# A bias carried in the idle rows of another matmul: forget-gate rows moved into the second score pass of a two-layer attention trunk

## The chip, the cores and the metric

The kernel runs on one core of one Trainium2 chip. The metric is device time in microseconds for one execution of the whole program. Where a difference is told in per cent, it is a difference of medians of such times.

## The reference, cut to what matters

Two layers run over 512 tokens of width 1024. Each layer projects the residual stream into four groups of heads (4 heads of width 64 each), mixes tokens in each group, normalises and projects the result back, and then applies a gated feed-forward block. The group that matters here is A, forgetting attention: a causal softmax whose score for query t and key s has the sum of the log forget gates between s and t added to it.

```python
log_f = jax.nn.log_sigmoid(fgate + fox_b_f[l])
cum = jnp.cumsum(log_f, axis=1).transpose(0, 2, 1)
...
s = jnp.einsum('bqhd,bkhd->bhqk', qi, k) * scale
s = s + cq[..., :, None] - cum_log_f[..., None, :]
s = jnp.where(kpos[None, :] <= qpos[:, None], s, NEG_INF)
p = jax.nn.softmax(s, axis=-1)
```

Groups B (latent attention), C (stick-breaking attention) and D (windowed attention) have no such bias.

## The kernel before, in words

**Precision by splitting.** Every matmul operand is held as a high part, rounded to the matmul's input type, and a low part, the remainder. A product of two such numbers takes three partial products: high by high, high by low, low by high.

**Scores in two passes.** A head is 64 wide and the TensorE array has 128 rows, so groups A, C and D pack two of the partial products into one pass. A q tile holds the high part of head i on rows 64i to 64i+63 and the low part on the other 64 rows. A `k` tile holds the low part of k against q's high part, and the high part of k against q's low part: the first pass gives both mixed products. A `kh` tile holds the high part of k on the head's own 64 rows and zeros on the other 64: the second pass, with the same q tile as the other operand, gives high by high. The zeros are written once, at the start of the program (L2205). There are three `kh` tiles in a ring, and five pairs of heads in a layer use them in turn (one for D, two each for C and A).

**The third pass of group A.** `gates()` computes the running sum of log gates for the four heads and splits it. It leaves two 128-row tiles, `augq` and `augk`, with 32 rows for each head, whose product over those rows is the bias cum[t] - cum[s]. Four copies of `augq`, one a head (`augh0` to `augh3`, L1100, on GpSimd), keep only the rows of their head. `group_a()` hands `causal_group` an extra operand pair, and each block of scores gets one more matmul: `augh` of the head by `augk`.

**Blocks.** A causal head is scored in four query blocks of 128 queries against 128, 256, 384 and 512 keys, in three groups (b=0 has the first two blocks, b=1 the third, b=2 the fourth). Each group's first pass is followed by a pass that adds the mask (`maskb` by `identb`). Softmax follows on VectorE (row maximum, L1433), ScalarE (exponential, L1443) and GpSimd or ScalarE (scaling, L1418 or L1416), then a transpose on TensorE (L1555) and its evacuation (L1361, L442), and the product with v.

**The order of the work.** The program plans itself: a list scheduler with estimated costs picks, engine by engine, what is issued next, and every engine then runs its instructions in that order. Attention tasks come before dense work (projections) in priority, so dense matmuls fill TensorE where attention is not ready. `copy()` (L717) picks ScalarE or GpSimd, whichever the planner believes will end first. Score groups are started in the order D, C, A, B, and only the first of the list is looked at, so B's scores are not started before A's last.

**Pairs.** Heads 0 and 1 of A are pair 0 (`fq0`, `fk0`), heads 2 and 3 are pair 1 (`fq1`, `fk1`). In layer 0 the dense order has `fk0`, ..., `fq0`, ..., `fq1`, `fk1`, then the latent queries (`q`) and the output projections; in layer 1 `fq0` and `fk0` come earlier. `q_evac` (L911, L444) and `k_evac` (L924, L442, and `copy`) move a pair out of PSUM.

Of the kernel before, what the change touches and what calls it, by code (L numbers as in the profile page):

```python
# [25 lines left out]
ALU = mybir.AluOpType  # L26
# [3 lines left out]
P = 128  # L30
S = 512
# [15 lines left out]
GA, GB, GC, GD = range(4)  # L47
# [18 lines left out]
E_PE, E_ACT, E_DVE, E_POOL, E_SP = range(5)  # L66
# [8 lines left out]
NOW = (0.0,) * 5  # L75


def join(*deps):

    if any(x is None for x in deps):  # L80
        return None
    return tuple(map(max, zip(*deps))) if len(deps) > 1 else deps[0]
# [18 lines left out]
def c_pool(n):  # L101
    return 245.0 + 0.832 * n
# [17 lines left out]
class Sched:  # L120
# [9 lines left out]
    def spawn(self, gen, prio=0, order=None):  # L130
        self.n += 1
        self.step((gen, prio, self.n if order is None else order), None)
# [220 lines left out]
def trunk(ctx: ExitStack, tc: tile.TileContext, d):  # L353
    nc = tc.nc
    ACT, DVE, POOL, PE = nc.scalar, nc.vector, nc.gpsimd, nc.tensor
    engines = {E_ACT: ACT, E_DVE: DVE, E_POOL: POOL}
    sched = Sched()
    spawn = sched.spawn
# [47 lines left out]
    amask = const.tile([P, 10], F32, name="amask")  # L406
# [30 lines left out]
    f = f32  # L437
# [279 lines left out]
    def copy(out, in_, n, dep, prio=None, psum=None):  # L717

        e_ = sched.best(dep, (E_ACT, c_act(n, psum is not None)), (E_POOL, c_pool(n)))[0]
        e = yield Op(e_, c_act(n, psum is not None) if e_ == E_ACT else c_pool(n), dep, prio)  # L720
        if e_ == E_ACT:
            ACT.copy(out=out, in_=in_ if psum is None else psum)  # L722
        else:
            POOL.tensor_scalar(out=out, in0=f(in_), scalar1=1.0, scalar2=0.0, op0=ALU.mult, op1=ALU.add)
        return e
# [138 lines left out]
    def layer(l):  # L864
        w_in = d["w_in"][l]
        qk = {}
# [3 lines left out]
        at = {}  # L870
# [185 lines left out]
        def gates():  # L1056
            e = yield lambda: join(at["gate"].dep, at["vec"], r_u.ready(), r_temp.ready(2)) if "gate" in at and "vec" in at else None
            gate, bf = small["gate"], vec["bf"]
            u = r_u.take()
            t0, t1 = r_temp.take(), r_temp.take()  # L1060
            gp = u.tile
            e = yield Op(E_PE, 4 * 107.0, join(e, u.dep))
            for t in range(NT):
                PE.transpose(out=gp[:, t * P:(t + 1) * P], in_=gate[:, t].rearrange("p h c -> p (h c)"), identity=ident)
            small["gate_h"].give(e)
            lg = [t0.tile, t1.tile]
            a = yield Op(E_ACT, c_act(S, True, 1), join(e, t0.dep))
            ACT.activation(out=lg[0], in_=gp, func=AF.Abs, bias=bf)
            b = yield Op(E_DVE, c_dve(S) + 61.0, join(e, t1.dep))
            DVE.tensor_scalar(out=lg[1], in0=gp, scalar1=bf, scalar2=0.0, op0=ALU.add, op1=ALU.min)  # L1070
            u.give(join(a, b))
            a = yield Op(E_ACT, c_act(S, False), a)
            ACT.activation(out=lg[0], in_=lg[0], func=AF.Exp, scale=-1.0)
            a = yield Op(E_ACT, c_act(S, False, 1), a)
            ACT.activation(out=lg[0], in_=lg[0], func=AF.Ln, bias=ones[:, 0:1])
            e = yield Op(E_DVE, c_dve(S), join(a, b))
            DVE.tensor_tensor(out=lg[1], in0=lg[1], in1=lg[0], op=ALU.subtract)
            e = yield Op(E_DVE, c_dve(S, 2.083), e)
            DVE.tensor_tensor_scan(out=lg[0], data0=lg[1], data1=lg[1], initial=0.0, op0=ALU.add, op1=ALU.bypass)
            augq, augk = (sb.tile([P, S], F32R, name=n, tag=n, bufs=1) for n in ("augq", "augk"))  # L1080
            heads = [sb.tile([P, S], F32R, name=f"augh{h}", tag=f"augh{h}", bufs=1) for h in range(4)]
            a = yield Op(E_ACT, c_act(S, False), e)
            ACT.copy(out=augq, in_=lg[0])
            e = yield Op(E_DVE, c_dve(S), a)
            DVE.tensor_tensor(out=lg[1], in0=lg[0], in1=f(augq), op=ALU.subtract)
            e = yield Op(E_DVE, c_dve(S, 0.52), e)
            DVE.tensor_copy(lg[0], f(augq))
            for aug, k in ((augq, 0), (augk, 3)):
                e = yield Op(E_DVE, c_half(S), e)
                DVE.tensor_scalar(out=aug, in0=lg[0], scalar1=amask[:, k:k + 1], scalar2=amask[:, k + 2:k + 3], op0=ALU.mult, op1=ALU.add)  # L1090
                e = yield Op(E_DVE, c_dve(S) + 61.0, e)
                DVE.scalar_tensor_tensor(out=aug, in0=lg[1], scalar=amask[:, k + 1:k + 2], in1=f(aug), op0=ALU.mult, op1=ALU.add)
                if aug is augq:
                    q_done = e
            t0.give(e)
            t1.give(e)
            hs = []
            for h in range(4):
                g = yield Op(E_POOL, c_pool(S), q_done)
                POOL.tensor_scalar(out=heads[h], in0=f(augq), scalar1=amask[:, 6 + h:7 + h], scalar2=0.0, op0=ALU.mult, op1=ALU.add)  # L1100
                hs.append(g)
            small["aug"] = heads, augk
            at["aug"] = join(e, *hs)


        def kv_norm(dep):
# [272 lines left out]
        def qk_pairs(q, i, k, kh, half):  # L1379

            return ((q[:, i], k[:, half]), (q[:, i], kh[:, half]))
# [39 lines left out]
        def softmaxes(scale=None):  # L1421
            def normed(ps, blocks, w, dep):

                p, nb = w[0].tile, len(blocks)
                r = sm.tile([P, 8], F32, name="smx", bufs=8)
                sl, c = [], 0
                for _, n in blocks:
                    sl.append(slice(c, c + n * P))
                    c += n * P
                dep = join(dep, w[0].dep)  # L1430
                for j, s_ in enumerate(sl):
                    e = yield Op(E_DVE, c_dve(s_.stop - s_.start), dep)
                    DVE.tensor_reduce(out=r[:, j:j + 1], in_=ps.tile[:, s_], op=ALU.max, axis=AX, negate=True)  # L1433
                nm = 0
                if scale is not None:
                    i0 = blocks[0][0]
                    e = yield Op(E_DVE, 72.0, join(e, at["rsq"]))
                    DVE.tensor_tensor(out=r[:, 2:2 + nb], in0=r[:, 0:nb], in1=scale[:, i0:i0 + nb], op=ALU.mult)
                    nm = 2
                for j, s_ in enumerate(sl):  # L1440
                    i = blocks[j][0]
                    a = yield Op(E_ACT, c_act(s_.stop - s_.start, True, 2 if scale is None else 3), e)
                    ACT.activation(out=p[:, s_], in_=ps.tile[:, s_], func=AF.Exp, bias=r[:, nm + j:nm + j + 1],  # L1443
                                   scale=1.0 if scale is None else scale[:, i:i + 1], accum_out=r[:, 4 + j:5 + j])
                ps.give(a)
                e = yield Op(E_DVE, 75.0, a)
                DVE.reciprocal(out=r[:, 6:6 + nb], in_=r[:, 4:4 + nb])
                out = []
                for j, s_ in enumerate(sl):
                    out.append((yield from normalize(p[:, s_], r[:, 6 + j:7 + j], s_.stop - s_.start, e)))  # L1450
                return w[0], join(*out)
            return normed
# [132 lines left out]
        def use_qk(key, held, n, dep):  # L1585
            held = held if isinstance(held, tuple) else (held,)
            qk_uses.setdefault(key, Joint(n, lambda dep: [h.give(dep) for h in held])).add(dep)

        def operands_2(qn, kn, more=None):

            def operands(h):
                pair, i = divmod(h, 2)
                if ((qn, pair), i) not in qk or ((kn, pair), i) not in qk or (more and more not in at):
                    return None
                (q, a, half), ((k, kh), b, _) = qk[(qn, pair), i], qk[(kn, pair), i]
                return qk_pairs(q.tile, i, k.tile, kh.tile, half), join(a, b, at[more] if more else NOW)

            def free(h, dep):
                pair, i = divmod(h, 2)
                for n in (qn, kn):  # L1600
                    use_qk((n, pair), qk[(n, pair), i][0], 6, dep)

            return operands, free
# [3 lines left out]
            return causal_group(GC, operands, None, 1, stick, "c", "vc", 2, free)  # L1607

        def group_a():
            operands, free = operands_2("fq", "fk", "aug")  # L1610

            def extras(h, i, o):
                heads, augk = small["aug"]
                n = (i + 1) * P
                return [(o, heads[h][:, i * P:n], augk[:, :n])]

            return causal_group(GA, operands, extras, 0, softmaxes(), "a", "va", 1, free)

        def group_b():
            def operands(h):  # L1620
# [649 lines left out]
```

## Time and profile before

| | us |
|---|---|
| median of 3 runs | 1229.88 (1228.12 to 1230.49) |
| the profiled execution, whole | 1222.83 |
| its span, first to last instruction | 1221.0 |
| TensorE busy | 1186.2 (97%) |
| VectorE busy | 893.4 (73%) |
| ScalarE busy | 675.8 (55%) |
| GpSimd busy | 238.7 (20%) |

The profiled execution is one run; 1.83 us of it lie around the span, and it lies 7.05 us under the median of the three runs. Attention takes about 0 to 240 us and 610 to 845 us of the span, the two feed-forward blocks the rest. In the rows, PE is TensorE, DVE VectorE, ACT ScalarE and POOL GpSimd; all matmuls have line 464, so they are told apart by their operands.

### The profile page before, as it was taken

To read this page: it belongs to the slowest core of one execution; us is meant where nothing else is said; L and a number is where in the kernel's file an instruction comes from. 1 tells how busy PE (TensorE), PEld (TensorE's weight loads), DVE (VectorE), ACT (ScalarE), POOL (GpSimd) and SP (SyncE) were. 2 spreads that over 40 slices of the span, in tenths; PEclk is the share of its full clock that TensorE was granted. 3 is DMA by queue.
4 is the path that set the end of the run, shared out by engine and by line. 5 is a ranking of instruction groups with operands and counts; after the bars stand their busy time and mean duration, and the time that the engine had idled before them with its cause. 6 is when DMAs were issued, how large, how long until landed. Compare 5 with 4: busy or idle time off the path is not lost.

```text
span 1221.0 us, 20328 instructions
## 1 busy us (share of the span) xinstructions
PE 1186.2 (97%) x7669; PEld 1077.5 (88%) x7669; DVE 893.4 (73%) x1699; ACT 675.8 (55%) x1429; POOL 238.7 (20%) x245
## 2 busy tenths in 40 slices
PE   9999999989999999999999999999899999999996
PEld 7989878779999889998889888788799989899985
DVE  5669668799986548873665886788999956599626
ACT  4759759456654335552347687584655633256421
POOL 3552653400000000000035536643000000000001
PEclk9999999999999999999999999999999999999999
DMA  6312220413333243423233221303234341343341
GB/s 201 88 43 66 59 95 9 139 57 101 103 105 103 71 138 89 118 87 123 86 71 86 56 62 31 104 21 118 87 88 119 93 135 49 109 120 87 104 138 69
DMA packets 112162, 110.75 MB, mean 91 GB/s; under 512 B 9792, under 2 KB 94656, under 8 KB 112064
## 3 DMA queue, kind: packets, MB, share of 16 engines
q1 hardware_dynamic: 112064, 109.45, 30.0%
q8 instruction: 60, 0.98, 0.3%
q14 instruction: 38, 0.31, 0.1%
HBM read 107.34 MB, written 2.10 MB: 90 GB/s over the span
## 4 chain that ended last, share of the span: by engine, by line
PE 84%; DVE 9%; issue 3%; ACT 3%; DMA 1%; POOL 0%; SPq 0%; POOLq 0%; DVEq 0%; ACTq 0%
PE ps L464 81%; PE ps L1555 2%; DVE x_res L1741 1%; DVE qk L442 1%; DVE xT L442 1%; DVE pt L442 1%; DVE x_res L856 1%; PE ps L749 1%; DMA x_res<-in_x 1%; ACT xT L722 0%; DVE qk L444 0%; DVE temp L1304 0%; DVE augk L1090 0%; ACT kh L924 0%; PE ps L1695 0%
## 5 line engine op out<-in xcount | busy, mean ns | idle before, releaser
L464 PE MATMUL ps<-xT,w_hi 128*128 128x256 f32 (+1 forms) x1128 | 216.7, 320 | 0.0
L464 PEld LDWEIGHTS ps<-xT,w_hi 128*128 128x128 f32 x1128 | 163.2, 191 | 11.8
L464 PE MATMUL ps<-w_hi,qk 128*128 128x512 f32 (+1 forms) x560 | 171.1, 387 | 0.0
L464 PE MATMUL ps<-xT,w_lo 128*128 128x256 f32 (+1 forms) x888 | 166.5, 305 | 0.0
L722 ACT CAST w_hi<-w_raw 128x1024 fp32r<-128x1024 f32 (+2 forms) x86 | 88.0, 1023 | 109.4 <-PE ps L464 87.0
L442 POOL TENSOR_TENSOR w_lo<-w_raw,w_hi 128x1024 fp32r<-128x1024 f32 (+4 forms) x66 | 120.9, 1838 | 107.3 <-ACT w_hi L722 88.9
L442 DVE TENSOR_TENSOR w_lo<-w_raw,w_hi 128x1024 fp32r<-128x1024 f32 x47 | 57.6, 1225 | 111.5 <-ACT w_hi L722 111.4
L464 PEld LDWEIGHTS ps<-xT,w_lo 128*128 128x128 f32 x888 | 124.1, 192 | 7.5
L464 PEld LDWEIGHTS ps<-w_hi,qk 128*128 128x128 f32 x560 | 104.2, 188 | 20.8
L464 PE MATMUL ps<-w_hi,mix 128*128 128x512 f32 x352 | 110.0, 393 | 4.8 <-DVE xT L442 3.5
L464 PE MATMUL ps<-w_lo,qk 128*128 128x512 f32 (+1 forms) x280 | 108.1, 386 | 0.0
L1909 ACT COPY temp<-ps 128x256 f32<-128x256 f32 x120 | 44.8, 373 | 84.4 <-PE ps L464 83.9
L659 ACT CAST w_hi<-temp 128x512 fp32r<-128x512 f32 x78 | 48.3, 620 | 64.4 <-DVE temp L602 35.7
L770 POOL TENSOR_SCALAR x_res<-x_res 128x1024 f32<-128x1024 f32 x8 | 9.4, 1179 | 374.3 <-DVE lnst L838 357.2
L464 PEld LDWEIGHTS ps<-w_hi,mix 128*128 128x128 f32 x352 | 64.6, 188 | 18.5 <-issue 4.3
L442 DVE TENSOR_TENSOR w_hi<-temp,w_hi 128x512 fp32r<-128x512 f32 x78 | 53.4, 688 | 30.7 <-ACT w_hi L659 30.5
L659 ACT CAST w_lo<-temp 128x512 fp32r<-128x512 f32 x82 | 50.7, 621 | 43.4 <-DVE temp L602 26.0
L467 POOL TENSOR_TENSOR lnst<-lnst,mhalf 128x1 f32<-128x1 f32 x4 | 3.9, 984 | 362.0 <-DVE lnst L838 362.0
L464 PE MATMUL ps<-xT,qk 128*128 128x256 f32 x528 | 67.8, 287 | 3.2 <-DVE qk L442 3.2
L464 PE MATMUL ps<-w_lo,mix 128*128 128x512 f32 x176 | 69.0, 392 | 0.9 <-DVE pt L442 0.9
L464 PE MATMUL ps<-w_hi,xT 128*128 128x388 f32 (+1 forms) x256 | 68.9, 350 | 0.4 <-DVE qk L444 0.4
L464 PEld LDWEIGHTS ps<-xT,qk 128*128 128x128 f32 x528 | 65.3, 194 | 4.2 <-DVE qk L442 4.0
(233 smaller groups left out, 2701.6 us busy)
## 6 DMA issues: line engine op xcount, KB each, us to landing
w_raw<-in_w_down SPq DMA_DIRECT2D x44, 512.0 KB, 3.8
w_raw<-in_w_in SPq DMA_DIRECT2D x26, 512.0 KB, 3.7
w_raw<-in_w_gate SPq DMA_DIRECT2D x24, 512.0 KB, 3.7
w_raw<-in_w_up SPq DMA_DIRECT2D x24, 512.0 KB, 3.7
w_raw<-in_w_o SPq DMA_DIRECT2D x16, 512.0 KB, 3.7
vd<-in_w_up SPq DMA_DIRECT2D x10, 512.0 KB, 3.7
mixf<-in_w_up SPq DMA_DIRECT2D x10, 512.0 KB, 3.6
vd<-in_w_gate SPq DMA_DIRECT2D x10, 512.0 KB, 3.8
```

Source lines behind the costliest of these rows:

```text
L442: eng.tensor_tensor(out=lo, in0=src, in1=f(hi), op=ALU.subtract)
L464: PE.matmul(out, lhsT=lhsT, rhs=rhs, start=start, stop=stop, skip_group_check=True)
L467: POOL.tensor_tensor(out=out, in0=ve, in1=mhalf[:ve.shape[0], :ve.shape[1]], op=ALU.pow)
L659: ACT.copy(out=self.part[0], in_=src)
L722: ACT.copy(out=out, in_=in_ if psum is None else psum)
L749: PE.transpose(out=u.tile[:, k * P:(k + 1) * P], in_=x[:, t, kk * P:(kk + 1) * P], identity=ident)
L770: POOL.tensor_scalar(out=x[:, t], in0=x[:, t], scalar1=ALPHA, scalar2=0.0, op0=ALU.mult, op1=ALU.add)
L856: DVE.scalar_tensor_tensor(out=x[:, t, csl], in0=centred[c], scalar=st[:, 9:10], in1=bb[c], op0=ALU.mult, op1=ALU.add)
L1555: PE.transpose(out=u.tile[:, k * P:(k + 1) * P], in_=p.tile[:, k * P:(k + 1) * P], identity=ident)
L1741: DVE.scalar_tensor_tensor(out=x[:, t, csl], in0=ps.tile, scalar=rs[:, t:t + 1], in1=x[:, t, csl], op0=ALU.mult, op1=ALU.add, accum_out=st ...
L1909: ACT.copy(out=dst, in_=src)
```

## The change

The third pass of group A is taken out. Its rows go where the second pass had zeros: each head gets its own query tile for the second pass (`augh` of the head) with the high part of q on the head's 64 rows and the masked gate rows of its pair on the other 64, and the zero rows of the pair's `kh` tile are overwritten with the pair's 64 rows of `augk`. That takes, a head, one masked copy on GpSimd over 64 rows instead of 128, and two plain copies of 64 rows by 512 (`copy`, on ScalarE or GpSimd). The copies wait for the pair's q and k. The heads are prepared in order, inside `gates()`. When all six score groups of a pair are issued, a new task writes the zeros back with two memsets on GpSimd, and only then is `kh` given back to its ring.

```diff
             t0.give(e)
             t1.give(e)
-            hs = []
+            small["aug"] = heads
             for h in range(4):
-                g = yield Op(E_POOL, c_pool(S), q_done)
-                POOL.tensor_scalar(out=heads[h], in0=f(augq), scalar1=amask[:, 6 + h:7 + h], scalar2=0.0, op0=ALU.mult, op1=ALU.add)
-                hs.append(g)
-            small["aug"] = heads, augk
-            at["aug"] = join(e, *hs)
+                pair, i = divmod(h, 2)
+                mine, other = slice(i * 64, i * 64 + 64), slice(64 - i * 64, 128 - i * 64)
+                from_ = slice(pair * 64, pair * 64 + 64)
+                q = yield Op(E_POOL, c_pool(S), q_done)
+                POOL.tensor_scalar(out=heads[h][other], in0=f(augq[from_]), scalar1=amask[from_, 6 + h:7 + h], scalar2=0.0,
+                                   op0=ALU.mult, op1=ALU.add)
+                yield lambda: NOW if (("fq", pair), i) in qk and (("fk", pair), i) in qk else None
+                (qt, dq, _), ((_, kh), dk, _) = qk[("fq", pair), i], qk[("fk", pair), i]
+                a = yield from copy(heads[h][mine], qt.tile[mine, i], S, dq)
+                b = yield from copy(kh.tile[other, i], augk[from_], S, join(dk, e))
+                at["aug", h] = join(q, a, b)
...
         def group_a():
-            operands, free = operands_2("fq", "fk", "aug")
-
-            def extras(h, i, o):
-                heads, augk = small["aug"]
-                n = (i + 1) * P
-                return [(o, heads[h][:, i * P:n], augk[:, :n])]
-
-            return causal_group(GA, operands, extras, 0, softmaxes(), "a", "va", 1, free)
+            plain, _ = operands_2("fq", "fk")
+
+            def operands(h):
+                if ("aug", h) not in at or plain(h) is None:
+                    return None
+                pairs, dep = plain(h)
+                return (pairs[0], (small["aug"][h], pairs[1][1])), join(dep, at["aug", h])
+
+            def zeros(pair, held, dep):
+                k, kh = held
+                for i in range(2):
+                    e = yield Op(E_POOL, 470.0, dep)
+                    POOL.memset(f(kh.tile[64 - i * 64:128 - i * 64, i]), 0.0)
+                k.give(dep)
+                kh.give(e)
+
+            uses = {}
+
+            def free(h, dep):
+                pair, i = divmod(h, 2)
+                use_qk(("fq", pair), qk[("fq", pair), i][0], 6, dep)
+                held = qk[("fk", pair), i][0]
+                uses.setdefault(pair, Joint(6, lambda dep: spawn(zeros(pair, held, dep)))).add(dep)
+
+            return causal_group(GA, operands, None, 0, softmaxes(), "a", "va", 1, free)
```

`operands_2` loses its third argument, which only group A used.

## Rows read from the trace of the kernel before

**Rows 1.** The page's chain that ended last, shares of the span by engine.

```profile
PE 84%; DVE 9%; issue 3%; ACT 3%; DMA 1%; POOL 0%; SPq 0%; POOLq 0%; DVEq 0%; ACTq 0%
```

**Rows 2.** Tile `augh`, its matmuls: count, ns min/median/max, starts, forms.

```profile
L464 PE MATMUL ps<-augk,augh x32: 279/362/478, 136.6 to 792.1; 128*128 128x128 f32 x8, 128*128 128x256 f32 x8, 128*128 128x384 f32 x8, 128*128 128x512 f32 x8
```

**Rows 3.** Timeline of PE, group C scoring: start, duration, line, operands, shape, count.

```profile
91.32 0.30 PE L464 MATMUL ps<-qk,qk 128*128 128x128 f32 x1
...
91.94 0.62 PE L464 MATMUL ps<-xT,w_hi 128*128 128x512 f32 x2
...
99.27 0.40 PE L464 MATMUL ps<-qk,qk 128*128 128x512 f32 x1
...
99.86 0.54 PE L464 MATMUL ps<-w_hi,xT 128*128 128x416 f32 x2
```

**Rows 4.** Timeline of PE, group A scoring heads 0 and 1 in layer 0.

```profile
137.89 0.39 PE L464 MATMUL ps<-qk,qk 128*128 128x512 f32 x1
...
138.70 0.60 PE L1151 MATMUL ps<-ident,temp 128*128 128x128 f32 x4
139.06 0.31 PE L464 MATMUL ps<-qk,qk 128*128 128x128 f32 x1
...
139.91 0.63 PE L464 MATMUL ps<-xT,w_hi 128*128 128x512 f32 x2
```

**Rows 5.** Windows, layer 0: length; busy PE, PEld, DVE, ACT, POOL; clock; DMA; GB/s.

```profile
136.00:172.00 36.00, 36.00 (x204) 30.91 (x203) 20.64 (x49) 24.69 (x60) 20.45 (x24) 0.95 0.26 83
172.00:185.40 13.40, 11.08 (x57) 8.61 (x56) 13.16 (x20) 7.38 (x14) 7.27 (x5) 1.00 0.25 82
185.40:222.00 36.60, 35.34 (x227) 30.27 (x228) 31.10 (x94) 31.13 (x87) 16.64 (x24) 1.00 0.09 28
```

**Rows 6.** Timeline of PE where A's pairs begin, in brackets idle before and releaser.

```profile
136.37 0.31 PE L464 MATMUL ps<-qk,qk 128*128 128x128 f32 x1
...
172.07 0.30 PE L464 MATMUL ps<-qk,qk 128*128 128x128 f32 x1
...
175.15 0.63 PE L464 MATMUL ps<-qk,w_hi 128*128 128x512 f32 x2
...
183.22 0.70 PE L464 MATMUL ps<-w_hi,mix 128*128 128x512 f32 x2 [1.75 <-DVE xT L442]
```

**Rows 7.** Timeline of DVE at the ends of `fq0` and `fk1`, layer 0.

```profile
135.51 1.41 DVE L444 SCALAR_TENSOR_TENSOR qk<-ps,qk 64x512 fp32r<-64x512 f32 x2 [1.19 <-ACT qk L911]
...
171.24 1.41 DVE L442 TENSOR_TENSOR qk<-ps,kh 64x512 fp32r<-64x512 f32 x2 [4.04 <-ACT kh L924]
...
176.21 0.29 DVE L1433 TENSOR_REDUCE smx<-ps 128x1 f32<-128x128 f32 x1
```

**Rows 8.** Timeline of ACT in layer 1, evacuation of `fk0`.

```profile
704.18 1.17 ACT L924 CAST kh<-ps 64x512 fp32r<-64x512 f32 x2
```

**Rows 9.** Timeline of PE in layer 1, head 0 of group A.

```profile
730.10 0.31 PE L464 MATMUL ps<-augk,augh 128*128 128x128 f32 x1
```

**Rows 10.** Tile `kh`: the copies on POOL.

```profile
L724 POOL TENSOR_SCALAR qk<-kh x17: 612/617/671, 18.0 to 775.0; 64x512 fp32r<-64x512 f32 x17
```

**Rows 11.** Timeline of POOL, a memset.

```profile
125.97 0.53 POOL L1120 MEMSET temp<- 128x512 f32 x1
```

**Rows 12.** Timeline of DVE, one operation twice in `gates()`.

```profile
63.11 0.54 DVE L1090 TENSOR_SCALAR augq<-temp,amask 128x512 fp32r<-128x512 f32 x1
...
65.64 2.75 DVE L1090 TENSOR_SCALAR augk<-temp,amask 128x512 fp32r<-128x512 f32 x1
```

**Rows 13.** Timeline of POOL beside it.

```profile
65.69 2.41 POOL L442 TENSOR_TENSOR w_lo<-w_raw,w_hi 128x1024 fp32r<-128x1024 f32 x1 [9.02 <-ACT w_hi L722]
68.07 3.31 POOL L1100 TENSOR_SCALAR augh<-augq,amask 128x512 fp32r<-128x512 f32 x4
```

**Rows 14.** Windows of 2 us, the granted clock after POOL.

```profile
152.00:154.00 2.00, 2.00 (x10) 1.90 (x9) 0.17 (x1) 0.00 (x0) 1.91 (x3) 0.50 0.72 219
154.00:156.00 2.00, 2.00 (x10) 1.73 (x9) 1.17 (x2) 1.53 (x4) 1.94 (x2) 0.74 0.11 43
```

More of the change, by code (lines that the diff above doesn't have):

```diff
@@ L1587, in use_qk, with operands_2 @@
             qk_uses.setdefault(key, Joint(n, lambda dep: [h.give(dep) for h in held])).add(dep)
-        def operands_2(qn, kn, more=None):
+        def operands_2(qn, kn):
             def operands(h):
                 pair, i = divmod(h, 2)
-                if ((qn, pair), i) not in qk or ((kn, pair), i) not in qk or (more and more not in at):
+                if ((qn, pair), i) not in qk or ((kn, pair), i) not in qk:
                     return None
                 (q, a, half), ((k, kh), b, _) = qk[(qn, pair), i], qk[(kn, pair), i]
-                return qk_pairs(q.tile, i, k.tile, kh.tile, half), join(a, b, at[more] if more else NOW)
+                return qk_pairs(q.tile, i, k.tile, kh.tile, half), join(a, b)
             def free(h, dep):
```

## The prediction, made before the changed kernel ran

> **What bounds the kernel now.** I read the chain that ended last first: 84% of it is TensorE, 9% VectorE, 3% ScalarE [rows 1]. A change that only takes matmuls away therefore starts with a good claim to its time, if the matmuls stand where TensorE is the one that sets the pace. So the second view is the windows of the stretch in which group A is scored [rows 5]. There are three kinds of stretch. From 136 to 172 us TensorE is busy in all of 36.00 us, while VectorE has 20.64 and ScalarE 24.69: pair 0 is scored here, and TensorE is the bound. From 172 to 185.4 us TensorE has 11.08 of 13.40 and VectorE 13.16: pair 1 becomes ready here, and VectorE is the bound (it still has the rotary products of group B to do). From 185.4 to 222 us TensorE has 35.34 of 36.60, with VectorE and ScalarE at 31 each: TensorE again, but closely followed. Layer 1 repeats this at the end of its attention. The third view is the timeline of TensorE and VectorE where the two pairs begin [rows 6, 7], because the new copies stand exactly there.
>
> **What is removed.** The third pass is 32 matmuls in the whole program, 8 of each width [rows 2]. Their listed durations overlap with their neighbours, so I don't add those up. I compare start to start, the same score group with and without the pass. Group C has none: its b=0 group runs from 91.32 to the next matmul at 91.94, 0.62 us, and its b=2 group from 99.27 to 99.86, 0.59 us [rows 3]. Group A's b=0 group runs from 139.06 to 139.91, 0.85 us, and b=2 from 137.89 to 138.70, 0.81 us [rows 4]. So the pass costs 0.23 us in b=0 (widths 128 and 256 together) and 0.22 us in b=2 (width 512). For b=1 (width 384) I take 0.17 us, an estimate three quarters of the way to the 512 figure. That is 0.62 us a head, and 8 heads give 5.0 us of TensorE time.
>
> **Which part of it counts.** Pair 0 in each layer lies where TensorE is saturated: 2 heads x 0.62 x 2 layers = 2.5 us, counted in full. Pair 1 is split. The whole of head 2 and the b=0 group of head 3 (0.62 + 0.23 = 0.85 us a layer) lie between 172 and 185.4 us, where TensorE has 2.3 us of idle time and at 183.22 us stands 1.75 us waiting for VectorE [rows 5, 6]. What is saved there becomes more waiting, so I count nothing; if it did count, it would be 1.7 us more. The rest of head 3 (0.39 us a layer) lies in the last stretch and is counted: 0.8 us. Sum: 3.3 us, with 5.0 us as its upper end and 2.5 us as its lower.
>
> **What is added: work.** Two copies a head are 16 copies of 64 x 512. The nearest rows are 0.61 us on GpSimd [rows 10] and 0.58 us on ScalarE (half of 1.17 for two, from PSUM, while these read SBUF) [rows 8]; I take 0.61. Eight memsets of 64 x 512 have as their nearest row one of 128 x 512 with 0.53 us [rows 11]. Together that is 9.8 + 4.2 = 14.0 us spread over two engines. The masked copies stay at four a layer. No instruction is added on TensorE or VectorE. In 172 to 185.4 us ScalarE is busy for 7.38 and GpSimd for 7.27 of 13.40 us [rows 5], in 136 to 172 us they have 11 and 15 us free: that free time hides the copies. The memsets come behind a pair's last score group; the `kh` tile they hold back is needed next by a later layer or by nobody, so they delay only what GpSimd has behind them. For work I charge nothing. If GpSimd's cover were gone, a memset pair in front of a softmax scaling would cost that score group up to 1.1 us, once a pair.
>
> **What is added: waits.** Today a pair is scored the moment its operands are there. `fq0` leaves VectorE between 135.51 and 136.92, and head 0 begins at 136.37; `fk1` leaves it between 171.24 and 172.65, and head 2 begins at 172.07 [rows 6, 7]. After the change two copies come in between, one issued behind the other: 1.2 us later if both run on one engine, about 0.6 us if on two. Head 1 and head 3 come behind a masked copy (0.8 us, a fourth of the 3.31 us at 68.07 [rows 13]) and two more copies: another 2.0 us at most. What would TensorE do meanwhile? In both places dense matmuls are ready: at 139.91 a projection of the residual stream [rows 4], at 175.15 the latent queries [rows 6], which now run behind the scores and can run ahead of them. And the scores of head 2 are not used at once: VectorE takes its first row maximum at 176.21 [rows 7], 4.1 us after the scores begin. So I price the wait at nothing; bare, it is 1.2 + 2.0 = 3.2 us a pair. In layer 1 pair 0 has no wait at all: `fk0` is being evacuated at 704.18 and head 0 begins at 730.10 [rows 8, 9]. That leaves three exposed pairs, 9.6 us if nothing covered them. A gain from this reordering is possible too (VectorE doing the rotary products before the two row maxima), but no more than those two small maxima, some 0.6 us a layer; I leave it inside the range.
>
> **Port between VectorE and GpSimd.** The same VectorE operation takes 0.54 us at 63.11 and 2.75 us at 65.64 [rows 12], when GpSimd begins a 2.41 us subtraction at 65.69 [rows 13]: it ends with that subtraction. The price of such a meeting is nearly the length of the GpSimd operation. The Trainium skill, in "GPSIMD Engine Reference", section 1 (Specifications), says that GpSimd shares its SBUF interfaces with VectorE and contends with VectorE instructions that take two SBUF inputs or run in a two-port mode; the trace agrees. That speaks against this change, which puts up to 24 more operations on GpSimd. Worked out from rows: an operation of 0.53 to 0.61 us can hold VectorE up by about 0.5 us, and between 172 and 185.4 us, where VectorE is the bound, I count two operations a layer that read SBUF alone: 2.0 us in all if each meets one. Elsewhere VectorE mostly reads PSUM, so I charge nothing in the forecast and make this a rival.
>
> **The sum.** The profiled execution took 1222.83 us, 1221.0 of span and 1.83 around it. Minus 3.3 gives 1219.5. The median of the three runs is 1229.88, 7.05 us more than that execution; I carry the difference over: 1226.6 us, 0.27% faster. About 0.2%, 2.5 us, is what a measurement of this kernel can tell from no change, so the forecast lies only just beyond it.
>
> **The rivals.**
>
> *All of it counts, and the clock helps.* In layer 0, after the tiny one-column matmuls of 148 to 151.5 us, the granted clock falls to 0.50 and 0.74 in two windows [rows 14]; that is the 1.2 GHz level for all of the first and about half of the second, and it gives away 1.0 + 0.5 = 1.5 us. If the new order pulls these matmuls apart and the full 5.0 us count, the gain is 6.5 us: 1223.4. For it: layer 1 runs the same work there without that fall. Against it: nothing in the change touches those matmuls. Chance 0.12.
>
> *Half of it is lost to a new fall of the clock.* The mirror case: a new order brings such a stretch into layer 1, for 1.5 us. 3.3 - 1.5 = 1.8 us gain: 1228.1, within 0.2%. Chance 0.15.
>
> *GpSimd holds VectorE up.* 3.3 - 2.0 = 1.3 us gain: 1228.6, within 0.2%. For it: the meeting at 65.64. Against it: short operations, few exposed places. Chance 0.14.
>
> *The copies become TensorE's wait.* TensorE takes its instructions in the planned order; if the plan puts the scores in front of the dense matmuls and the copies land late (GpSimd at that time has subtractions of 2.4 us in its queue, and a copy behind one is late by that much), everything behind the scores stands. With three exposed pairs at 3.2 us that is 9.6 - 5.0 = 4.6 us slower: 1234.5. It decides from 7.5 us of waits on, 2.5 a pair. For it: the scores start today within 0.9 us of their operands, so no slack was there. Against it: the planner knows the copies and has dense work to put first. Chance 0.17.
>
> **How the numbers follow.** The forecast's own case (a gain of 2.5 to 5.0 us) has 0.42. Faster by over 0.2%: 0.42 + 0.12 = 0.54. Within 0.2%: 0.15 + 0.14 = 0.29. Slower: 0.17. The range goes from 1223.0, just under the best rival, to 1231.0, which is above both rivals of no change and leaves out the slower one with its 0.17. The forecast's own range is 1224.9 to 1227.4.
>
> **What would show it.** No matmul reads `augk` and `augh` together; a b=0 group of A takes 0.62 us start to start and a b=2 group 0.59. The stretch that answers to 136 to 172 us still has TensorE busy throughout and is shorter by about 1.2 us. At pair 1 the latent queries start before head 2's scores, and TensorE shows no wait of over 0.5 us on a copy into `augh` or `kh`. The prediction is wrong if that wait is there, if VectorE operations next to GpSimd's copies or memsets grow from 0.7 us towards 1.3, or if other windows than today's show a granted clock near 0.5.

## The result, and the profile after

The changed kernel takes 1230.2 us (median of 22 runs, 1226.8 to 1237.45); the kernel before, 22 times on the same chips, 1224.41 us (1219.97 to 1230.82). The ratio is 1.0049, interval 1.0035 to 1.0063: **0.49% slower**, about 6 us, where 0.27% faster was forecast. The three runs shown for the kernel before, 1228.12 to 1230.49, were from the upper end of its spread; the forecast in us stood on their median, so it is the gain that has to be compared, not the time.

The first things to look for are those that the change does by itself. Tile `augh` in the trace after (count, ns min/median/max, starts, forms):

```profile
L464 PE MATMUL ps<-kh,augh x32: 282/362/482, 137.7 to 800.8; 128*128 128x128 f32 x8, 128*128 128x256 f32 x8, 128*128 128x384 f32 x8, 128*128 128x512 f32 x8
L1103 POOL TENSOR_SCALAR augh<-augq,amask x8: 687/695/743, 68.0 to 783.4; 64x512 fp32r<-64x512 f32 x8
L722 ACT CAST augh<-qk x5: 617/619/623, 137.6 to 784.6; 64x512 fp32r<-64x512 f32 x5
L724 POOL TENSOR_SCALAR augh<-qk x3: 612/612/622, 134.9 to 710.8; 64x512 fp32r<-64x512 f32 x3
```

The 32 matmuls of the third pass [rows 2] are gone and the second pass reads `augh`. The copies take 0.61 to 0.62 us on either engine, as charged. Group A's scores, from TensorE's timeline after, to be held against [rows 4]:

```profile
139.07 0.39 PE L464 MATMUL ps<-qk,qk 128*128 128x512 f32 x1
...
139.66 0.22 PE L464 MATMUL ps<-qk,qk 128*128 128x128 f32 x1
...
732.22 0.22 PE L464 MATMUL ps<-qk,qk 128*128 128x128 f32 x1
...
732.75 0.63 PE L464 MATMUL ps<-pt,v 128*128 128x512 f32 x2
```

A b=2 group takes 0.59 us start to start, as foreseen, and a b=0 group 0.53, where 0.62 was foreseen. Part of that is its place: directly behind another score group, as here, a b=0 group took 0.77 us before, from the row below to 175.15 in [rows 6]. So the pass cost 0.24 us there, close to the 0.23 of the prediction. From the timeline before:

```profile
174.38 0.22 PE L464 MATMUL ps<-qk,qk 128*128 128x128 f32 x1
```

No matmul waits for a copy. At pair 1 five of the six groups of latent-query matmuls run ahead of head 2's scores, where three did before, as foreseen.

Then, where the time went. I cut both executions at the same five events, which leave four stretches: the first matmul on `xT`, the first latent-query matmul of layer 0, the zero fill of the gates in layer 1, the first latent-query matmul of layer 1, the end of VectorE's work. Windows before (length; busy PE, PEld, DVE, ACT, POOL; granted clock; DMA; GB/s):

```profile
10.28:169.82 159.54, 158.00 (x908) 140.20 (x905) 105.23 (x213) 112.23 (x264) 78.07 (x82) 0.98 0.29 79
169.82:644.15 474.33, 464.10 (x3124) 425.65 (x3123) 355.94 (x679) 245.22 (x499) 49.49 (x50) 1.00 0.31 93
644.15:773.41 129.26, 126.69 (x727) 112.11 (x726) 89.50 (x171) 91.64 (x220) 70.01 (x70) 1.00 0.25 68
773.41:1217.47 444.06, 430.13 (x2873) 394.04 (x2871) 336.17 (x623) 222.05 (x441) 38.93 (x40) 1.00 0.30 94
```

and after:

```profile
10.11:168.27 158.16, 156.47 (x899) 137.67 (x898) 104.93 (x213) 114.62 (x268) 78.87 (x83) 0.99 0.29 77
168.27:645.02 476.75, 465.62 (x3116) 425.67 (x3115) 357.83 (x679) 248.90 (x506) 48.72 (x51) 0.99 0.31 93
645.02:780.42 135.40, 129.41 (x720) 113.67 (x718) 88.16 (x171) 93.96 (x222) 69.58 (x73) 0.96 0.23 65
780.42:1224.60 444.18, 430.21 (x2865) 394.19 (x2863) 336.86 (x623) 224.16 (x445) 39.73 (x42) 0.99 0.31 94
```

The first stretch gains 1.4 us, the second loses 2.4, the third **6.1**, the fourth nothing. In the third TensorE has seven matmuls fewer in the trace and is busy 2.7 us longer: its clock fell from 1.00 to 0.96. So each execution is best split into three: TensorE's waits (the idle times in brackets of its timeline, added up), the time given away by the clock (one minus the granted clock, times TensorE's busy time, over windows of 2 us), and the rest, which is its work. A low clock while TensorE stands is left out, because the stand is counted already.

| profiled execution | the four stretches | waits | clock | rest |
|---|---|---|---|---|
| before | 1207.2 | 21.7 | 5.1 | 1180.4 |
| after | 1214.5 | 25.9 | 10.4 | 1178.2 |

The rest fell by 2.2 us. Waits took 4.2 us and the clock 5.3 us, 9.5 us in all. In the third stretch the split closes by itself: waits 5.9 us against 2.5, clock 3.9 against none, and 1.2 us less of work, which is what the two heads scored there were priced at (2 x 0.62). What the new order did to TensorE's work in the other stretches is not separated here.

That the clock takes this much does not hang on one profile. The mean granted clock is 0.9863 over the 22 executions of the changed kernel, and 0.9919 to 0.9924 over the executions of the kernel before that ran beside the experiments. One minus this, times the span, gives 16.8 us against 9.3 to 9.9: an estimate, and an upper one, since it counts stands and the ends of the span too.

Waits and clock have their largest part at one place. TensorE's timeline after, layer 1:

```profile
759.32 1.72 PE L464 MATMUL ps<-ones,temp 128*128 128x1 f32 x14 [1.15 <-ACT temp L1233]
762.85 0.80 PE L464 MATMUL ps<-qk,w_hi 128*128 128x512 f32 x1 [0.78 <-ACT qk L455]
765.38 0.80 PE L464 MATMUL ps<-qk,w_hi 128*128 128x512 f32 x1 [1.74 <-DVE qk L444]
```

and its windows there, the clock after POOL:

```profile
760.00:762.00 2.00, 2.00 (x18) 1.73 (x17) 0.21 (x2) 0.63 (x2) 1.62 (x4) 0.93 0.00 0
762.00:764.00 2.00, 0.87 (x2) 0.29 (x1) 1.74 (x2) 0.80 (x2) 2.00 (x2) 0.50 0.00 0
764.00:766.00 2.00, 0.62 (x2) 0.53 (x3) 1.33 (x2) 0.00 (x0) 1.84 (x3) 0.50 0.24 43
766.00:768.00 2.00, 2.00 (x7) 1.63 (x6) 0.15 (x1) 1.24 (x3) 1.94 (x2) 0.50 0.56 219
768.00:770.00 2.00, 2.00 (x15) 1.91 (x15) 1.94 (x4) 1.96 (x5) 0.00 (x1) 0.86 0.00 0
```

3.7 us of stands and, counted as above, 2.2 us of clock (at 0.50 TensorE runs at its 1.2 GHz level): 5.9 us. The kernel before has no stand between 750 and 775 us. The matmuls that wait at 762.85 and 765.38 build the latent group's keys; they wait for the normalized latent vector, and that is late from its first step on. ScalarE's timeline, the squares of group C's finish (L1495 before, L1501 after) and of the key norm (L1114, L1120), before:

```profile
742.95 0.31 ACT L1114 ACTIVATE temp<-temp 128x128 f32<-128x128 f32 x1
...
748.68 1.19 ACT L1495 ACTIVATE temp<-mixf 128x512 f32<-128x512 f32 x2
```

and after, in the other order:

```profile
748.98 1.22 ACT L1501 ACTIVATE temp<-mixf 128x512 f32<-128x512 f32 x2
...
753.04 0.31 ACT L1120 ACTIVATE temp<-temp 128x128 f32<-128x128 f32 x1
```

Both want `temp` tiles, of which there are seven: the key norm three at once (`kv_norm`: `yield lambda: r_temp.ready(3)`), the finish two. In the plan of the kernel before the key norm comes first; in the plan made for the changed kernel the finish and then the second latent query half take theirs, and the key norm starts 10.1 us later. Nothing in the diff touches either. That is the theory (the hand-out of scratch tiles); its rival is that the copies and fills cost the time themselves.

### The profile page after: what moved, and what is told of

The parts are those of the page before. It is cut to its first block, busy times and chain, and to the rows that moved or that the text cites. A ratio compares the mean times of both kernels' runs of the same rounds, so it can differ in the third digit from the quotient of the medians.

```text
span 1227.8 us, 20275 instructions
## 1 busy us (share of the span) xinstructions
PE 1188.5 (97%) x7637; PEld 1076.4 (88%) x7637; DVE 894.4 (73%) x1699; ACT 686.3 (56%) x1446; POOL 239.1 (19%) x252
## 4 chain that ended last, share of the span: by engine, by line
PE 81%; DVE 11%; ACT 4%; issue 3%; DMA 1%; SPq 0%; POOL 0%; POOLq 0%; DVEq 0%; ACTq 0%
PE ps L464 79%; PE ps L1561 2%; DVE x_res L1764 1%; DVE xT L442 1%; DVE pt L442 1%; DVE qk L442 1%; DVE smx L1439 1%; ACT pt L1367 1%; DVE x_res L856 1%; ACT temp L1449 1%; DMA x_res<-in_x 1%; DVE qk L444 1%; PE ps L749 0%; DVE augk L1090 0%; DVE temp L1310 0%
## 5 line engine op out<-in xcount | busy, mean ns | idle before, releaser
L722 ACT CAST w_hi<-w_raw 128x1024 fp32r<-128x1024 f32 (+2 forms) x89 | 91.3, 1026 | 108.5 <-PE ps L464 87.3
```

## The experiments

All ratios are to the kernel before on the same chip, five rounds, with 95% intervals. They are not quotients of the plain medians, from which they differ by up to 0.0017.

**1. The changed kernel with the old hand-out.**

```diff
             h, h2, h3 = (r_temp.take() for _ in range(3))
+            at["kv_temps"] = NOW
...
-            yield lambda: join(r_mix.ready(), r_temp.ready(2))
+            yield lambda: join(r_mix.ready(), r_temp.ready(2)) if g != GC or "kv_temps" in at else None
```

> The changed kernel with one more condition: group C's finish takes its two scratch tiles only after the key norm of the latent group has its three. If the hand-out of scratch tiles in layer 1 is what cost 7.0 us between 712 and 780 us, the key norm's squares come back from 753 to about 744 us, the stand of TensorE at 759 to 767 us and its fall of the clock go, and the whole takes 5 to 7 us less than the changed kernel: 0.995 to 0.999 of the kernel before. If the copies and zero fills themselves cost the time, it stays at 1.004 to 1.006 of the kernel before.

Measured: 1.0011 [0.9995, 1.0028], 1226.62 us. 4.7 us of the 6 come back; the ratio is above the 0.995 to 0.999 put down. The key norm's squares stand at 742 us again, and TensorE has two short waits where it had three long ones:

```profile
756.21 0.49 PE L464 MATMUL ps<-qk,w_hi 128*128 128x512 f32 x1 [0.22 <-ACT qk L455]
757.00 0.50 PE L464 MATMUL ps<-qk,w_hi 128*128 128x512 f32 x1 [0.29 <-DVE qk L444]
```

One fall of the clock stays there (0.50 at 760 to 762 us). So the hand-out holds, and it is not everything: this kernel is still not faster than the one before.

**2. The kernel before with the new hand-out.**

```diff
-            yield lambda: r_temp.ready(3)
+            yield lambda: r_temp.ready(3) if l == 0 or "c_temps" in at and 1 in cq_ else None
...
             q = [r_temp.take(), r_temp.take()]
+            if g == GC:
+                at["c_temps"] = NOW
```

> The kernel before, third pass and all, with the mirrored condition: in layer 1 the key norm takes its three scratch tiles only after group C's finish and the second latent query half have theirs. No copy, no zero fill, all matmuls stay. If the hand-out is the cause, it is slower by 5 to 7 us (1.004 to 1.006) and shows the key norm's squares near 752 us and a window near half clock behind 758 us. If the copies and fills are the cause, it stays within 0.1% of the kernel before.

Measured: 1.0037 [1.0019, 1.0054]: 4.5 us slower, without one copy, just under the range put down. The third stretch of its profile is 133.5 us against 129.3, with 4.8 us of waits against 2.5; that execution (1224.42 us) was the fastest of its twelve.

**3. The third pass not emitted, the order kept** (the planner still counts it).

```diff
-                        qk_mm(o, pairs, i, n * P, c == 0, [masks(ps.tile, b)] * (c == 0) + extras(h, i, o))
+                        qk_mm(o, pairs, i, n * P, c == 0, [masks(ps.tile, b)] * (c == 0))
```

> The kernel before with its plan kept instruction for instruction, but the 32 matmuls of the third pass of group A not emitted (the forget gates' bias is left out of the scores). What it saves is what the pass is worth with every order held: by the prediction's sum 3.3 us, 5.0 at most, 2.5 at least: 0.9959 to 0.9980 of the kernel before. If the saving is eaten by waits for VectorE wherever it falls, less than 1.5 us: over 0.9988.

Measured: 0.9981 [0.9966, 0.9996]: 2.3 us. The prediction counted 3.3; the interval (0.5 to 4.2 us) holds that, and just not the full 5.0.

**4. The pass out of the planner's costs too, no copies.** On top of experiment 3:

```diff
-            return causal_group(GA, operands, extras, 0, softmaxes(), "a", "va", 1, free)
+            return causal_group(GA, operands, None, 0, softmaxes(), "a", "va", 1, free)
```

> The kernel before with the third pass left out of the planner's costs and of the program (the forget gates' bias is left out of the scores), and no copies and no zero fills in its place. The plan made without the pass hands the scratch tiles to group C's finish first, as the changed kernel's does. If the hand-out is the cause, the 3 to 5 us that the pass gives are lost again and some more: 1.001 to 1.004 of the kernel before, with the key norm's squares in layer 1 near 750 us and the stand of TensorE behind them. If the copies and fills are the cause, it is as fast as the pass allows: 0.996 to 0.998.

Measured: 1.0000 [0.9986, 1.0014], between the two expectations: 2.3 us are lost against experiment 3 by the order alone, though the two intervals overlap. The key norm is late here too (its POOL memset at 752.0 us, 743.6 before), with 5.8 us of waits in the third stretch. Leaving the pass out is enough to flip the hand-out.

**5. The changed kernel's order, copies and fills not emitted.** `copy` and `zeros` plan their operations here and issue none.

```diff
-                return (pairs[0], (small["aug"][h], pairs[1][1])), join(dep, at["aug", h])
+                return pairs, join(dep, at["aug", h])
```

> The changed kernel with its plan kept instruction for instruction, but the 16 copies and the 8 zero fills not emitted (group A's second pass reads the plain queries, so the forget gates' bias is left out of the scores). If the copies and fills cost time by themselves, as the 3 to 6 us between the kernels with and without them suggest, it is 0.999 to 1.002 of the kernel before. If only the order of the plan costs, it stays at 1.0035 to 1.006, as the changed kernel.

Measured: 1.0028 [1.0014, 1.0042], between the two. The order alone costs 5.7 us against experiment 3, which does the same work but for masked copies of twice the rows; the copies at most the 2.6 us up to 1.0049, and the two intervals overlap. Its three stands in layer 1 are those of the changed kernel, 1.15, 0.83 and 1.79 us.

**6. Any other order.** A constant of the planner in the kernel before.

```diff
-SLACK = 30.0
+SLACK = 29.0
```

> The kernel before with one constant of its planner changed from 30 to 29, which computes the same with the same instructions in another order (some 600 lines of TensorE's order differ). If a re-plan alone moves the time by some us, whatever it is for, it lies outside 0.999 to 1.001 of the kernel before, up to 1.004. If only the named hand-out matters (the key norm keeps its place here), it is within 0.1%.

Measured: 1.0019 [1.0007, 1.0031]. A re-plan without any purpose costs 2.3 us, with the key norm in its place.

**7. The old hand-out, copies and fills on ScalarE.** On top of experiment 1:

```diff
-                a = yield from copy(heads[h][mine], qt.tile[mine, i], S, dq)
-                b = yield from copy(kh.tile[other, i], augk[from_], S, join(dk, e))
+                a = yield Op(E_ACT, c_act(S, False), dq)
+                ACT.copy(out=heads[h][mine], in_=qt.tile[mine, i])
+                b = yield Op(E_ACT, c_act(S, False), join(dk, e))
+                ACT.copy(out=kh.tile[other, i], in_=augk[from_])
```

and the fills as activations with scale 0.

> The first experiment's kernel with all 16 copies and the 8 zero fills planned on ScalarE, none on GpSimd. If what the copies and fills still cost there is GpSimd holding VectorE up, it comes to 0.998 to 0.9995 of the kernel before. If the cost is the wait for the copies or the order, it stays at 1.000 to 1.003, as the first experiment.

Measured: **0.9976 [0.9964, 0.9988]**, 1221.64 us: faster than both kernels, by 2.9 us and by 8.6 us, and below both ranges put down. What made it so is for the next ones to tell.

**8. The third pass twice.** The order is kept.

```diff
                     for o, a, b in extra:
                         mm(o, a, b, start=False, stop=False)
+                        if a is not identb:
+                            mm(o, a, b, start=False, stop=False)
```

> The kernel before with its plan kept, and each of the 32 matmuls of the third pass emitted twice (the bias counts double). If TensorE is the bound where they stand, 5.0 us more: 1.0041 (1.003 to 1.005). If taking the pass away gave only 2.3 us because half of it stands where VectorE is the bound, doubling it costs 2.3 to 3.3 us as well: 1.0019 to 1.0027. If more work on TensorE keeps its clock up, less than that.

Measured: 1.0012 [0.9998, 1.0025]: 1.5 us for 5.0 us of matmuls. That is the third expectation's number and not its reason: in the profile the clock gives away 8.3 us against 5.1, and the mean granted clock is 0.9911 against 0.9921, so the added work did not keep it up. The waits are 16.9 us against 21.7. The 1.75 us for VectorE at pair 1 ([rows 6] has the one of layer 0) are gone in both layers: the added matmuls run in time in which TensorE stood anyway.

**9. The mirror of 7: copies and fills on GpSimd.** The same for `b`; the fills as in the change.

```diff
-                a = yield from copy(heads[h][mine], qt.tile[mine, i], S, dq)
+                a = yield Op(E_POOL, c_pool(S), dq)
+                POOL.tensor_scalar(out=heads[h][mine], in0=f(qt.tile[mine, i]), scalar1=1.0, scalar2=0.0, op0=ALU.mult, op1=ALU.add)
```

> The first experiment's kernel with all 16 copies and the 8 zero fills planned on GpSimd, none on ScalarE: the mirror of the one with all on ScalarE, which came to 0.9976 of the kernel before. If the engine of the copies decides (GpSimd holds VectorE up, or has its copies behind long subtractions), it is slower than the mixed one's 1.0011: 1.002 to 1.004. If the gain with all on ScalarE was the luck of one order, this one may fall anywhere within 0.997 to 1.004, also below 1.000.

Measured: 1.0000 [0.9990, 1.0011], 2.9 us behind experiment 7 but not behind the mixed one. The first expectation fails; the second is so wide that it could hardly fail, and says little.

**10. Experiment 7 without the condition of experiment 1.**

```diff
-            yield lambda: join(r_mix.ready(), r_temp.ready(2)) if g != GC or "kv_temps" in at else None
+            yield lambda: join(r_mix.ready(), r_temp.ready(2))
```

> All copies and fills on ScalarE, but without the condition that gives the key norm its scratch tiles first; in this plan it gets them late in layer 1, as in the changed kernel. If the hand-out costs 4.6 us whatever the copies do, 0.9976 becomes 1.001 to 1.003. If the hand-out mattered only together with the copies on GpSimd, it stays below 0.999.

Measured: 1.0030 [1.0017, 1.0044]: the hand-out costs 6.6 us here, with all copies on ScalarE. In its third stretch the clock gives away 7.4 us.

**11. Experiment 7's order without copies and fills.** The operands as in experiment 5, the fills left out likewise, and

```diff
-                ACT.copy(out=heads[h][mine], in_=qt.tile[mine, i])
...
-                ACT.copy(out=kh.tile[other, i], in_=augk[from_])
```

> The plan of the kernel with the key norm first and all copies and fills on ScalarE, kept instruction for instruction, with neither copies nor fills emitted (the second pass reads the plain queries, so the forget gates' bias is left out). If copies on ScalarE are covered, as the prediction charged them, it is at the same 0.9976, within 0.0010. If ScalarE's copies cost as much as the mixed ones, it is 2 us faster still: 0.9955 to 0.9965.

Measured: 0.9974 [0.9958, 0.9990] against 0.9976: on ScalarE no cost of theirs shows. The intervals leave room for some 2 us, and by plain medians (0.9957 and 0.9977) experiment 11 is 2.4 us ahead, so that a small cost is not excluded.

**12. Copies on ScalarE, fills on GpSimd.** Experiment 7 with

```diff
-                    e = yield Op(E_ACT, c_act(S, False), dep)
-                    ACT.activation(out=kh.tile[64 - i * 64:128 - i * 64, i], in_=f(kh.tile[64 - i * 64:128 - i * 64, i]), func=AF.Copy, scale=0.0)
+                    e = yield Op(E_POOL, 470.0, dep)
+                    POOL.memset(f(kh.tile[64 - i * 64:128 - i * 64, i]), 0.0)
```

> The key norm first, the 16 copies on ScalarE, the 8 zero fills on GpSimd: between the kernel with all on ScalarE (0.9976) and the mixed one (1.0011). If the fills are what GpSimd holds VectorE up with, near 1.000; if it is the copies, or the order they stand in, near 0.998.

Measured: 0.9979 [0.9964, 0.9994]: fills on GpSimd cost nothing that shows.

**13 and 14. The orders of experiments 1 and 9 without copies and fills**, planned and not issued, with the operands as in experiment 5.

> The first experiment's plan (key norm first, copies mixed over ScalarE and GpSimd, 1.0011) kept instruction for instruction, with neither copies nor fills emitted (the forget gates' bias is left out of the scores). If its copies and fills cost time by themselves, it comes down to 0.9975 to 0.9990. If it is the order of that plan, it stays at 1.000 to 1.002.

> The plan with all copies and fills on GpSimd (1.0000) kept, with neither copies nor fills emitted (the bias is left out). If GpSimd's copies cost time by themselves, 0.9965 to 0.9980, as far below as the copies cost; if the order does, 0.9995 to 1.0005.

Measured: 13: 1.0009 [0.9988, 1.0030] against 1.0011 with them; here no cost of the copies shows, within some 3 us, and the order is what is left. 14: 0.9971 [0.9955, 0.9987] against 1.0000, without overlap; here the copies cost 3.5 us. The trace tells a part of how. GpSimd at pair 1 of layer 0, experiment 9:

```profile
172.23 0.61 POOL L1108 TENSOR_SCALAR augh<-qk 64x512 fp32r<-64x512 f32 x1
...
175.75 4.74 POOL L442 TENSOR_TENSOR w_lo<-w_raw,w_hi 128x1024 fp32r<-128x1024 f32 x2
```

experiment 14, where the mask of head 3 alone stands ahead of the subtraction:

```profile
171.92 2.40 POOL L442 TENSOR_TENSOR w_lo<-w_raw,w_hi 128x1024 fp32r<-128x1024 f32 x1
```

and TensorE in experiment 9, the waits of both layers that experiment 14 doesn't have:

```profile
178.19 0.50 PE L464 MATMUL ps<-w_lo,mix 128*128 128x512 f32 x1 [0.69 <-POOL w_lo L442]
...
783.46 0.50 PE L464 MATMUL ps<-w_lo,mix 128*128 128x512 f32 x1 [0.69 <-POOL w_lo L442]
```

Four copies and the mask take GpSimd from 172.23 to 175.75 us, in front of the low half of an output weight, and the output projection waits for it. In all, experiment 9 has 4.2 us more of waits than 14 (21.7 and 17.5), with the clock's part equal (8.3 and 8.4). The two waits shown are 1.4 us of that; another 1.3 us stand at the start of the feed-forward blocks, where none of the copies is, and how they follow from the copies is not shown.

## Why the prediction was wrong

**The step that failed** is the last of its pricing: the sum takes the new program for the old one with some terms changed, and of reordering the sum says only that a gain from it is possible, "no more than those two small maxima, some 0.6 us a layer; I leave it inside the range". A loss from a new order stands only among the rivals, as one fall of the clock for 1.5 us.

The order is not a constant here. The planner makes it anew from the costs, and a small difference flips who gets a scratch tile. Six kernels that all lack the pass and the copies, and differ almost by their order alone (in four of them the masked copies have half the rows), came to 0.9971, 0.9974, 0.9981, 1.0000, 1.0009 and 1.0028 (experiments 14, 11, 3, 4, 13, 5): 7 us, more than twice the gain that was forecast. The sum of the change in measured terms: pass out with the order held -2.3 us (experiment 3), the new order +5.7 (experiment 5 against 3), copies and fills +2.6 with intervals that overlap: +6.0.

The largest known piece of the order's part is the hand-out: 4.7 us by experiment 1, 4.5 by 2, 6.6 by 10, and 2.3 with intervals that overlap between 5 and 13, where no copies run. Each of these pairs also has two different plans behind the hand-out, so none is its price alone. The traces show its direct part: in the third stretch TensorE waits 2.5 to 2.9 us in all eleven profiles in which the key norm comes early, and 4.8 to 6.0 us in the five in which it comes late (the changed kernel, 2, 4, 5 and 10). The rest of the order's cost is not put down to single places.

**What was removed** was somewhat large at 5.0 us: with the order held, TensorE's work falls by 3.6 us without the pass (1180.4 to 1176.8, experiment 3) and grows by 4.3 us with the pass twice (1184.7, experiment 8). **Which part counts** was 3.3 and measured 2.3, with an interval that holds both. The reason given, that pair 1's share turns into waiting for VectorE, is not what experiment 3 shows: its waits are 20.3 us against 21.7, and in place of the 1.75 us at 183.22 it has 0.52 and 0.98. A part of what was saved shows up as clock: 11.9 us against 5.1 in the profile, and by the mean granted clock of all executions (0.9897 against 0.9919) 12.6 against 9.9 us, an estimate as above. So the size was near, partly by luck. The reverse case, more work that fills the waits, is what experiment 8 shows.

**Work of the copies at nothing** held on ScalarE as far as the intervals tell (11 against 7), and for the fills (12). On GpSimd it held in one order and failed in another: nothing that shows in 1 against 13, 3.5 us in 9 against 14. The prediction looked for VectorE held up and for late copies; the one victim that the trace shows is a weight's low half behind them. For the changed kernel itself, where seven of the 16 copies are on GpSimd, the 2.6 us are not settled: its waits repeat those of experiment 5 at the same places, and what differs between the two profiles is the clock (10.4 and 7.4 us).

**Waits at nothing** was right: no wait on a copy, in any pair. The rival of the slower side (the copies become TensorE's wait) had the sign and not the mechanism.

**The port.** The price per meeting was about right, the place wrong. (In [rows 12, 13] the operation ends at 68.39, 0.29 us behind the subtraction's 68.10, and not with it.) In the stand at 765.38 a VectorE operation of four numbers a row starts beside a subtraction on GpSimd, and the low half of the latent vector waits behind it; first GpSimd's timeline after, then VectorE's:

```profile
762.30 2.35 POOL L442 TENSOR_TENSOR w_lo<-w_raw,w_hi 128x1024 fp32r<-128x1024 f32 x1
```

```profile
762.87 1.81 DVE L1246 TENSOR_SCALAR rsq<-ssq 128x4 f32<-128x4 f32 x1
764.59 0.74 DVE L444 SCALAR_TENSOR_TENSOR qk<-ps,gkv,qk 128x512 fp32r<-128x512 f32 x1
```

In the kernel before the same operation takes 0.17 us in layer 0 and 2.36 us in layer 1, at 764.0, where nobody waits for it. The Trainium skill, "GPSIMD Engine Reference", section 1 (Specifications), says that the two engines share SBUF interfaces; the trace agrees, with the operation ending where the subtraction ends (764.68 and 764.65). Layer 0 has its like: `smx` at 210.51 takes 2.23 us beside a subtraction of 2.37, and TensorE stands 1.50 us at 214.56 for the block behind it. None of these meetings involves a copy of the change; the order brought them together.

**The clock** was a rival with one fall at 1.5 us. A fall gives away 1.7 us where TensorE works through it, and the profile after has seven such shares against three before, two of them at 760 to 770. That the signs named for a wrong prediction included other windows near 0.5 was to the point: 686 to 690 us shows 0.66 and 0.50, where the kernel before has 1.00.

## What to carry to other kernels

Where a planner or a scheduler makes the order, a change of a few us can't be priced term by term alone: first compare the two orders, look for whoever takes several of a shared buffer at once (three scratch tiles here), and hold the order fixed to measure the term. Give the chain that others wait for its buffers by a rule and not by a tie; here the kernels with and without that one condition lie 2.3 to 6.6 us apart, and together with the copies on ScalarE it turned a loss of 0.49% into a gain of 0.24%. Before putting small work on an engine with room, name what is queued behind it: copies of 0.6 us showed no cost on ScalarE, and 3.5 us in all on GpSimd, where some stand in front of weight subtractions.

## What the runs showed that was not expected

The clock's falls are partly chance. The kernel before shows 0.50 and 0.74 at 152 to 156 us [rows 14], and experiment 3 falls there as well; experiment 2 has the same instructions up to there and stays at 1.00, and its first stretch is 2.9 us shorter. Its windows there, the clock after POOL:

```profile
152.00:154.00 2.00, 2.00 (x14) 1.74 (x13) 1.23 (x2) 1.97 (x5) 1.84 (x3) 1.00 0.55 207
154.00:156.00 2.00, 2.00 (x15) 1.82 (x14) 1.71 (x3) 1.94 (x6) 1.94 (x2) 1.00 0.00 0
```

Nor does the length of a stand tell: here are the sums of group D's finish, before and after, with 0.95 us of waiting and no fall behind it, and with 0.70 us and the fall at 686.

```profile
683.72 1.72 PE L464 MATMUL ps<-ones,temp 128*128 128x1 f32 x14 [0.95 <-ACT temp L1495]
```

```profile
684.34 1.72 PE L464 MATMUL ps<-ones,temp 128*128 128x1 f32 x14 [0.70 <-ACT temp L1501]
```

The Trainium skill, "TensorE: Matmul & The Clock Gate", section "HAM oscillation — how this bites in real kernels", describes a kernel that loses its clock again and again in the DMA waits between its tiles; the falls behind the stands at 759 to 766 us agree with that, the pair of rows above is not told apart by it. Single executions of one kernel spread over 10 us, and the granted clock goes with the time: of the 35 executions of the kernel before beside experiment 1, the fastest (1220.06 us) had 0.997 and the slowest (1230.67 us) 0.985. Differences of 2 us need the many runs that stand behind these intervals.
